# Reordering the opening loads of a one-core hybrid decoder step: three tiles of x, the first weights, then the rest of x

## Chip, cores and metric

The kernel runs on one core of one Trainium2 chip. The metric is the device time of one launch in microseconds (us); the median of several runs counts. The engines are TensorE (PE, with its weight loads PEld), VectorE (DVE), ScalarE (ACT), GpSimd (POOL) and SyncE (SP), which here only issues transfers.

## What is computed

One inference step of a one-layer decoder with two head groups (sparse attention and HGRN2), for a prompt of 1024 tokens and 8 sample tokens that share the weights. What matters here is only its beginning:

```
def _rmsnorm(x, g):
    x32 = x.astype(jnp.float32)
    y = x32 * lax.rsqrt(jnp.mean(x32 * x32, axis=-1, keepdims=True) + EPS)
    return (y * g.astype(jnp.float32)).astype(x.dtype)

z = _split(_rmsnorm(x, g_pre) @ w_in)     # x: (1024 + 8) x 1024, w_in: 1024 x 3864
f = lb + (1.0 - lb) * jax.nn.sigmoid(z['f_b'])
q = jax.nn.silu(z['q_b'])
```

`lb` is a softmax over `hg_lower`, two small rows of 512 numbers. Everything is float32.

## The kernel before

**Stages.** `project` loads and normalizes x, then makes ten products of x with slices of `w_in`, with the HGRN2 work between them; `attention` and `finish` follow. A float32 product is made of three products of rounded parts: x is split into `xhi` and `xlo`, each weight tile into `w_hi` and `w_lo`, and the products hi*hi, hi*lo and lo*hi are added up in PSUM.

**x.** `load_x` is a generator. It issues the loads of nine tiles (eight of 128 tokens with 1024 columns, 512 KB each, and one of 8 tokens), the first four into the later tile `V`, the others into `x_in` (tags AT, S and O of the HGRN pool). For each tile, ACT squares it and sums the squares (L200), DVE works out the inverse root in a chain of twelve operations on one column (L202, L79 to L84; `x_ss`, `rs_t`, `rs_g`, `x_rs`) and scales the tile (L214), TensorE transposes it in two halves of four 128x128 blocks (L218, two PSUM buffers `ph`), and ACT and DVE write `xhi` (L50) and `xlo` (L51). The sum of the next tile is asked for before the scaling of the present one.

**Weights.** `load_w` makes eight tiles (k = 0 to 7) of 128 rows and up to 512 columns: one transfer per column part into `w_raw` (three buffers), `w_hi` on ACT (L238), `w_lo` on DVE (L239). Tile k is loaded when buffer k - 3 has been split. The first product uses two parts of 256 columns, so sixteen transfers of 128 KB.

**First product.** `feat(..., groups_first=True)`: 4 feature blocks of 128 (two of f, two of q) in each of 3 token groups of 344 tokens, 24 matmuls of 344 columns each. Its evacuations allocate tiles F and K (two buffers each) and Q; F's needs `lb` and `oml`, which `consts2` works out from `hg_lower` (L145 to L154, tiles `hg_lo`, `hg_mx`, `hg_ex`). The transfers of `hg_lower`, issued by ACT, are put after the last x transfer in the order.

**Order of the work.** No engine's order is written by hand. A planner runs the program against a simulated clock, with the program's order as priority, and fixes the order of the instructions of each engine and of the issues of each queue; on the chip each engine keeps that order and waits in it. `after` only adds an order between two instructions. The page table (`pt_raw`, L648, eight transfers of 4-byte elements) belongs to a later part of the program.

Of the kernel before, what the change touches and what calls it, by code (L numbers as in the profile page):

```python
# [7 lines left out]
F32 = mybir.dt.float32  # L8
# [4 lines left out]
AF = mybir.ActivationFunctionType  # L13
OP = mybir.AluOpType
# [7 lines left out]
TS = T + NB  # L22
D = 1024
EPS = 1e-6
C_Q, C_KC, C_KS, C_KW, C_G, C_ZA, C_QB, C_FB, C_IB, C_ZB = 0, 512, 768, 1024, 1280, 1304, 1816, 2328, 2840, 3352


class Kernel:
# [148 lines left out]
    def load_x(self, ctx):  # L177
        nc, a = self.nc, self.a
        self.xhi = self.xpool.tile([128, 8, TS], F32R, name="xhi")
        self.xlo = self.xpool.tile([128, 8, TS], F32R, name="xlo")  # L180
        wk = self.pool(ctx, "xwork", bufs=2)
        xs, hp = [], self.hp
        four = hp.tile([128, 8, 512], F32, name="V", bufs=1).rearrange("p a b -> p (a b)")
        for i in range(9):
            n = 128 if i < 8 else NB
            if i < 4:
                x = four[:, i * D:(i + 1) * D]
            else:
                x = hp.tile([128, 8, 128], F32, name="x_in", tag=("AT", "S", "O")[(i - 4) // 2]).rearrange("p a b -> p (a b)")[:n]
            self.xdma = nc.sync.dma_start(x, a["x_prompt"][0, i * 128:i * 128 + n] if i < 8 else a["x_sample"][:, 0])  # L190
            xs.append((i, n, x))

        def norms(tiles):
            ss = wk.tile([128, 4], F32, name="x_ss")
            if tiles[-1] == 8:
                nc.gpsimd.memset(ss, 1.0)
            for j, t in enumerate(tiles):
                _, n, x = xs[t]
                junk = wk.tile([128, D], BF, name="x_sq")[:n]
                nc.scalar.activation(junk, x, AF.Square, accum_out=ss[:n, j:j + 1])  # L200
            ss = ss[:, :len(tiles)]
            nc.vector.tensor_scalar(ss, ss, 1.0 / D, EPS, op0=OP.mult, op1=OP.add)  # L202
            r = wk.tile([128, 4], F32, name="x_rs")[:, :len(tiles)]
            self.rsqrt(wk, r, ss)
            return r

        groups = [(i,) for i in range(9)]
        r = norms(groups[0])
        for gi, tiles in enumerate(groups):
            rn = norms(groups[gi + 1]) if gi + 1 < len(groups) else None  # L210
            for j, t in enumerate(tiles):
                i, n, x = xs[t]
                tok = slice(i * 128, i * 128 + n)
                nc.vector.tensor_scalar(x, x, r[:n, j:j + 1], None, op0=OP.mult)  # L214
                for h in range(2):
                    p = self.ps_h.tile([128, 512], F32, name="ph").rearrange("p (a b) -> p a b", a=4)
                    for k in range(4):
                        nc.tensor.transpose(p[:, k, :n], x[:, (4 * h + k) * 128:(4 * h + k + 1) * 128], self.ident[:n, :n])  # L218
                    self.split(self.xhi[:, 4 * h:4 * h + 4, tok], self.xlo[:, 4 * h:4 * h + 4, tok], p[:, :, :n],
                               nc.scalar, nc.vector)  # L220
            r = rn
            yield gi

    def load_w(self, src, *parts):

        nc = self.nc
        out = []
        width = sum(p[1] for p in parts)
        for k in range(8):
            raw = self.wpool.tile([128, 512], F32, name="w_raw", bufs=3)[:, :width]  # L230
            o = 0
            for c0, n in parts:
                dma = nc.sync.dma_start(raw[:, o:o + n], src[k * 128:(k + 1) * 128, c0:c0 + n])
                o += n
            hi = self.wpool.tile([128, 512], F32R, name="w_hi", bufs=9)[:, :width]
            lo = self.wpool.tile([128, 512], F32R, name="w_lo", bufs=9)[:, :width]
            g = self.gpre[:, k:k + 1]
            nc.scalar.activation(hi, raw, AF.Copy, scale=g)  # L238
            nc.vector.scalar_tensor_tensor(lo, raw, g, hi.bitcast(F32), op0=OP.mult, op1=OP.subtract)  # L239
            out.append((hi, lo))  # L240
        self.nload += 1
        for b in range(2 * self.nload - 4, 2 * self.nload - 2):
            if 0 <= b < NB:
                self.after(nc.sync.dma_start(
                    self.a["win_kv_sample"][0, b, :511].rearrange("s a h d -> s (a h d)"),
                    self.a["cache_win_kv"][0, b, 1:].rearrange("s a h d -> s (a h d)")), dma)
        return out

    def feat(self, *parts, groups_first=False, w=None, ps=None):

# [29 lines left out]
    def project(self, ctx):  # L280
        nc, a = self.nc, self.a
# [5 lines left out]
        hp = self.hp = self.pool(hctx, "hg", bufs=2)  # L287
        with ExitStack() as c:
            self.gpre = self.xpool.tile([128, 8], F32, name="gpre")
            nc.scalar.dma_start(self.gpre, a["g_pre"][0].rearrange("(k p) -> p k", p=128))  # L290
            self.nload = 0
            x = self.load_x(c)
            next(x)
            w0 = self.load_w(a["w_in"][0], (C_FB, 256), (C_QB, 256))
            for _ in x:
                pass
            self.consts2(c, mp)
# [5 lines left out]
        K, Q, F = {}, {}, {}  # L303
# [338 lines left out]
    def page_index(self, pool):  # L642

        nc = self.nc
        pt = self.a["page_table"]
        raw = pool.tile([128, NB], I32, name="pt_raw", bufs=1)
        for i in range(8):
            dma = nc.sync.dma_start(raw[16 * i:16 * i + 16], bass.AP(tensor=pt.tensor, offset=pt.offset + i, ap=[[0, 16], [8, NB]]))  # L648
            if i == 0:
                self.pidma = dma  # L650
        lane = pool.tile([128, NB], I32, name="pt_lane", bufs=1)
        nc.gpsimd.iota(lane, pattern=[[0, NB]], base=0, channel_multiplier=1)
        nc.vector.tensor_scalar(lane, lane, 15, None, op0=OP.bitwise_and)
        self.pidx = self.cp.tile([128, NB], I32, name="pidx")
        nc.vector.scalar_tensor_tensor(self.pidx, raw, 16.0, lane, op0=OP.mult, op1=OP.add)
# [738 lines left out]
```

## Time and profile before

| | |
|---|---|
| median of 3 runs | 1091.31 us (1091.28 to 1093.86) |
| profiled execution | 1092.95 us, span 1091.2 us |
| PE busy | 1051.9 us (96%) |
| DVE, ACT, POOL busy | 618.0, 388.5, 241.1 us |
| mean transfer rate | 107 GB/s |

PE is the engine that is busy nearly all the time. Matmuls overlap, so the spacing of their starts, not the duration of one, tells their pace.

### The profile page before, as it was taken

How to read it: one execution, taken by the hardware profiler on the slowest of the kernel's cores; microseconds unless marked ns; L12 is line 12 of the kernel's file. 1: busy time of each engine (PE TensorE's matmuls, PEld its weight loads, DVE VectorE, ACT ScalarE, POOL GpSimd, SP SyncE). 2: the span in 40 equal slices, each digit the busy share in tenths (PEclk: the TensorE clock that was granted, in tenths of full speed). 3: DMA queues.
4: the chain of work that ended last, by engine and by line, in shares of the span. 5: the costliest groups of instructions: out<-in, count | busy, mean ns of one | idle time of the engine just before them, and what ended most of it. 6: DMA issues, size and time to landing. Idle time of an engine off the chain costs nothing.

```text
span 1091.2 us, 18921 instructions
## 1 busy us (share of the span) xinstructions
PE 1051.9 (96%) x7021; PEld 936.8 (86%) x7021; DVE 618.0 (57%) x1822; ACT 388.5 (36%) x786; POOL 241.1 (22%) x276
## 2 busy tenths in 40 slices
PE   4999999999899899999989999999999999999998
PEld 3898799999789899999968898888788888778876
DVE  6847565666484535543574666766655677461223
ACT  4622234313133335432224544553554332241112
POOL 0024231331031133002023111111323133131111
PEclk9999999999999999999969999999999999999999
DMA  6212023333454666304468711001831474131110
GB/s 195 78 29 68 11 72 100 117 101 120 144 173 135 193 222 208 135 1 118 123 186 250 189 38 42 20 21 41 230 111 42 137 199 119 41 97 49 47 37 31
DMA packets 119007, 116.44 MB, mean 107 GB/s; under 512 B 18902, under 2 KB 101166, under 8 KB 116612
## 3 DMA queue, kind: packets, MB, share of 16 engines
q1 hardware_dynamic: 97412, 79.46, 25.6%
q10 hardware_dynamic: 19200, 19.01, 5.1%
q0 software_dynamic: 2304, 16.78, 4.6%
q8 instruction: 55, 0.90, 0.4%
q14 instruction: 36, 0.29, 0.1%
HBM read 84.84 MB, written 29.31 MB: 105 GB/s over the span
## 4 chain that ended last, share of the span: by engine, by line
PE 81%; DMA 9%; DVE 5%; issue 2%; ACT 1%; POOL 1%; SPq 0%; ACTq 0%; DVEq 0%; POOLq 0%
PE pa L42 37%; PE pb L42 27%; PE ph L42 9%; PE pt L42 4%; DMA vb<-v_d 2%; DMA w_raw<-w_in 2%; PE ph L714 1%; DMA w1r<-cmp_w 1%; DMA fw_raw<-w_out 1%; PE pa L1124 1%; DMA f_z<-oT_d 1%; DMA cg<-cache_cmp_kv,pidx 1%; DMA V<-x_prompt 1%; PE ph L1318 1%; DVE w_lo L239 1%
## 5 line engine op out<-in xcount | busy, mean ns | idle before, releaser
L42 PEld LDWEIGHTS pb<-V,P 128*128 128x128 f32 x1056 | 143.8, 194 | 11.8 <-POOL P L959 0.9
L42 PE MATMUL pb<-V,P 128*128 128x128 f32 x1056 | 149.2, 279 | 0.5 <-DVE mx L908 0.4
L42 PE MATMUL pa<-xhi,w_hi 128*128 128x344 f32 x384 | 125.7, 329 | 3.3 <-ACT w_hi L238 1.7
L42 PE MATMUL pa<-xlo,w_hi 128*128 128x344 f32 x384 | 124.2, 325 | 0.0
L42 PE MATMUL pa<-xhi,w_lo 128*128 128x344 f32 x384 | 123.3, 326 | 0.0
L954 ACT ACTIVATE P<-ph 128x512 f32<-128x512 f32 (+4 forms) x148 | 85.8, 595 | 100.4 <-PE ph L42 78.3
L915 DVE CUSTOM_DVE_ANT_0 junk<-pa,mask 128x320 bf16<-128x320 f32 (+5 forms) x150 | 73.1, 496 | 35.7 <-PE pa L42 35.1
L42 PE MATMUL pa<-w_lo,xhi 128*128 128x256 f32 (+2 forms) x256 | 79.8, 316 | 0.1
L42 PE MATMUL pa<-w_hi,xlo 128*128 128x256 f32 (+2 forms) x256 | 79.6, 315 | 0.0
L42 PE MATMUL pa<-w_hi,xhi 128*128 128x256 f32 (+2 forms) x256 | 78.9, 317 | 0.0
L42 PEld LDWEIGHTS pa<-xhi,w_hi 128*128 128x128 f32 x384 | 73.3, 191 | 5.0 <-ACT w_hi L238 2.4
L238 ACT ACTIVATE w_hi<-w_raw,gpre 128x512 fp32r<-128x512 f32 (+2 forms) x80 | 47.4, 616 | 78.1 <-DMA w_raw<-w_in 46.5
L42 PEld LDWEIGHTS pa<-xlo,w_hi 128*128 128x128 f32 x384 | 73.2, 191 | 0.1
L42 PEld LDWEIGHTS pa<-xhi,w_lo 128*128 128x128 f32 x384 | 72.7, 190 | 0.4 <-DVE w_lo L239 0.2
L42 PE MATMUL ph<-QA,KA 128*128 128x512 f32 (+4 forms) x148 | 66.4, 451 | 2.5 <-ACT P L954 2.5
L42 PE MATMUL pa<-KB,QB 65*128 65x320 f32 (+6 forms) x195 | 64.8, 369 | 1.1 <-DVE mx L915 0.7
L239 DVE SCALAR_TENSOR_TENSOR w_lo<-w_raw,gpre,w_hi 128x512 fp32r<-128x512 f32 (+2 forms) x80 | 51.4, 663 | 21.6 <-ACT w_hi L238 20.9
L42 PE MATMUL pa<-fw_hi,yh 128*128 128x512 f32 (+1 forms) x160 | 61.7, 385 | 0.0
L42 PE MATMUL pa<-fw_hi,yl 128*128 128x512 f32 (+1 forms) x160 | 61.6, 385 | 0.0
L42 PE MATMUL pa<-fw_lo,yh 128*128 128x512 f32 (+1 forms) x160 | 61.6, 385 | 0.0
L42 PE MATMUL ph<-QB,KB 68*128 68x512 f32 (+3 forms) x148 | 58.5, 405 | 0.0
L42 PE MATMUL pb<-x,w1h 128*128 128x384 f32 (+1 forms) x192 | 55.9, 353 | 0.3 <-ACT x L50 0.3
(457 smaller groups left out, 2391.3 us busy)
## 6 DMA issues: line engine op xcount, KB each, us to landing
w_raw<-w_in SPq DMA_DIRECT2D x32, 256.0 KB
w_raw<-w_in SPq DMA_DIRECT2D x48, 128.0 KB
VS<-sg SPq DMA_DIRECT2D x8, 512.0 KB
sg<-cache_win_kv SPq DMA_DIRECT2D x16, 256.0 KB
fw_raw<-w_out SPq DMA_DIRECT2D x16, 256.0 KB
fw_raw<-ple_gate SPq DMA_DIRECT2D x16, 256.0 KB
f_x<-x_prompt SPq DMA_DIRECT2D x8, 512.0 KB
win_kv_sample<-cache_win_kv SPq DMA_DIRECT2D x8, 511.0 KB
```

Of the source, the lines that this page charges most:

```text
L42: return self.nc.tensor.matmul(out, lhsT, rhs, start=start, stop=stop, skip_group_check=True)
L238: nc.scalar.activation(hi, raw, AF.Copy, scale=g)
L239: nc.vector.scalar_tensor_tensor(lo, raw, g, hi.bitcast(F32), op0=OP.mult, op1=OP.subtract)
L714: nc.tensor.transpose(pt[:, i * 128:(i + 1) * 128], src[b0 + j // 2, kv][:, j % 2, 2 * jp:2 * jp + 2].rearrange("p j d -> p (j d)"), self. ...
L915: nc.vector.tensor_tensor_reduce(junk, pm, mk, 1.0, -1e30, op0=OP.add, op1=OP.max, accum_out=o)
L954: nc.scalar.activation(P, ps, AF.Exp, scale=0.125)
L1124: nc.tensor.transpose(pt[:, j * 128:(j + 1) * 128], rows(j), self.ident)
L1318: nc.tensor.transpose(pt[:, c], h[:, k * 128:(k + 1) * 128], self.ident[:n, :n])
```

## The change

The x loads are issued in two parts with all sixteen first weight transfers between them. These weights go into four tiles of the HGRN pool that are not yet in use (tags F, F, K, K; two weight tiles in each). Tiles 1 and 2 of x share one norm. The first weights are split into hi and lo in two passes: 128 columns of all eight tiles, then 384 columns of all eight. The page-table transfers are put behind the last weight transfer that was issued before them in the program, which is that of the second product.

```diff
@@ load_x
                 x = hp.tile([128, 8, 128], F32, name="x_in", tag=("AT", "S", "O")[(i - 4) // 2]).rearrange("p a b -> p (a b)")[:n]
+            if i == 3:
+                yield
             self.xdma = nc.sync.dma_start(x, a["x_prompt"][0, i * 128:i * 128 + n] if i < 8 else a["x_sample"][:, 0])
             xs.append((i, n, x))
...
-        groups = [(i,) for i in range(9)]
+        groups = [(0,), (1, 2)] + [(i,) for i in range(3, 9)]
@@ load_w
-    def load_w(self, src, *parts):
+    def load_w(self, src, *parts, raws=None):
...
         for k in range(8):
-            raw = self.wpool.tile([128, 512], F32, name="w_raw", bufs=3)[:, :width]
-            o = 0
-            for c0, n in parts:
-                dma = nc.sync.dma_start(raw[:, o:o + n], src[k * 128:(k + 1) * 128, c0:c0 + n])
-                o += n
+            if raws:
+                raw = raws[k]
+            else:
+                raw = self.wpool.tile([128, 512], F32, name="w_raw", bufs=3)[:, :width]
+                o = 0
+                for c0, n in parts:
+                    dma = self.lastw = nc.sync.dma_start(raw[:, o:o + n], src[k * 128:(k + 1) * 128, c0:c0 + n])
+                    o += n
...
-            nc.scalar.activation(hi, raw, AF.Copy, scale=g)
-            nc.vector.scalar_tensor_tensor(lo, raw, g, hi.bitcast(F32), op0=OP.mult, op1=OP.subtract)
-            out.append((hi, lo))
+            if not raws:
+                nc.scalar.activation(hi, raw, AF.Copy, scale=g)
+                nc.vector.scalar_tensor_tensor(lo, raw, g, hi.bitcast(F32), op0=OP.mult, op1=OP.subtract)
+            out.append((hi, lo, raw, g))
+        for cs in ((slice(0, 128), slice(128, width)) if raws else ()):
+            for hi, lo, raw, g in out:
+                nc.scalar.activation(hi[:, cs], raw[:, cs], AF.Copy, scale=g)
+                nc.vector.scalar_tensor_tensor(lo[:, cs], raw[:, cs], g, hi[:, cs].bitcast(F32), op0=OP.mult, op1=OP.subtract)
...
-        return out
+        return [o[:2] for o in out]
@@ project
             next(x)
-            w0 = self.load_w(a["w_in"][0], (C_FB, 256), (C_QB, 256))
+
+            raws = []
+            for tag in ("F", "F", "K", "K"):
+                t = hp.tile([128, TS], F32, name="w0", tag=tag)
+                raws += [t[:, :512], t[:, 512:1024]]
+            for k, raw in enumerate(raws):
+                for o, c0 in ((0, C_FB), (256, C_QB)):
+                    nc.sync.dma_start(raw[:, o:o + 256], a["w_in"][0, k * 128:(k + 1) * 128, c0:c0 + 256])
+            for _ in range(2):
+                next(x)
+            w0 = self.load_w(None, (C_FB, 256), (C_QB, 256), raws=raws)
             for _ in x:
                 pass
@@ page_index
             dma = nc.sync.dma_start(raw[16 * i:16 * i + 16], bass.AP(tensor=pt.tensor, offset=pt.offset + i, ap=[[0, 16], [8, NB]]))
+            self.after(dma, self.lastw)
```

## Rows read from the trace of the kernel before

**Rows 1.** Busy time and share of the span, whole page.

```profile
PE 1051.9 (96%) x7021; PEld 936.8 (86%) x7021; DVE 618.0 (57%) x1822; ACT 388.5 (36%) x786; POOL 241.1 (22%) x276
```

**Rows 2.** Chain that ended last, first 70 us: start us, us, what.

```profile
2.19 8.22 DMA V<-x_prompt
...
20.75 7.21 DMA w_raw<-w_in
...
41.22 0.44 PE ph L218 x4
```

**Rows 3.** Busy windows of TensorE: stretch, length, busy, PEclk, DMA share, GB/s.

```profile
40.00:77.10 37.10, 37.10 (x244) 1.00 0.02 4
```

**Rows 4.** Timeline of TensorE: start us, us, line, operation.

```profile
21.04 1.23 PE L42 MATMUL pa<-xhi,w_hi 128*128 128x344 f32 x3 [1.00 <-ACT xhi L50]
...
24.21 0.49 PE L42 MATMUL pa<-xhi,w_lo 128*128 128x344 f32 x1
24.50 0.49 PE L42 MATMUL pa<-xhi,w_hi 128*128 128x344 f32 x1
...
25.39 0.32 PE L42 MATMUL pa<-xhi,w_hi 128*128 128x344 f32 x1
...
26.79 0.32 PE L42 MATMUL pa<-xhi,w_lo 128*128 128x344 f32 x1
28.82 0.42 PE L42 MATMUL pa<-xhi,w_hi 128*128 128x344 f32 x1 [1.71 <-ACT w_hi L238]
...
77.22 0.40 PE L42 MATMUL pa<-w_hi,xhi 128*128 128x512 f32 x1
```

**Rows 5.** Timeline of SP's queue: start us, us of issuing, transfer.

```profile
9.15 7.77 SPq L233 DMA_DIRECT2D w_raw<-w_in  x6
16.97 3.27 SPq L648 DMA_DIRECT2D pt_raw<-page_table  x7
20.36 63.76 SPq L233 DMA_DIRECT2D w_raw<-w_in  x18
```

**Rows 6.** Windows by transfer rate: last three columns PEclk, DMA share, GB/s.

```profile
2.00:8.00 6.00, 0.00 (x0) 0.00 (x0) 3.87 (x25) 2.98 (x6) 0.00 (x0) 1.00 0.83 260
8.00:14.00 6.00, 1.97 (x8) 1.57 (x8) 4.07 (x30) 2.83 (x8) 0.00 (x0) 1.00 1.03 408
14.00:17.00 3.00, 1.97 (x8) 1.55 (x8) 3.00 (x18) 1.51 (x4) 0.00 (x0) 1.00 1.05 237
18.50:25.50 7.00, 6.00 (x23) 4.87 (x23) 5.28 (x22) 3.58 (x8) 0.00 (x0) 1.00 0.05 0
```

**Rows 7.** Packets of all queues from 20 to 22 us.

```profile
DMA packets 235, 0.00 MB, mean 0 GB/s; under 512 B 235, under 2 KB 235, under 8 KB 235
```

**Rows 8.** Timeline of DVE: the norm chains of tiles 0 and 1.

```profile
8.16 0.15 DVE L202 TENSOR_SCALAR x_ss<-x_ss 128x1 f32<-128x1 f32 x1 [1.17 <-ACT x_sq L200]
...
9.38 0.16 DVE L84 SCALAR_TENSOR_TENSOR x_rs<-rs_t,rs_g 128x1 f32<-128x1 f32 x1
```

**Rows 9.** ACT's groups by form: count, busy us, mean ns, idle before.

```profile
L238 ACT ACTIVATE w_hi<-w_raw,gpre 128x512 fp32r<-128x512 f32 x16 | 11.0, 719 | 13.4 <-DMA w_raw<-w_in 13.4
L50 ACT CAST xhi<-ph 128x512 fp32r<-128x512 f32 x16 | 9.1, 581 | 4.3 <-PE ph L218 4.2
L601 ACT ACTIVATE o_sq<-O 128x128 bf16<-128x128 f32 x32 | 9.5, 299 | 0.2
L200 ACT ACTIVATE x_sq<-V 128x1024 bf16<-128x1024 f32 x4 | 4.2, 1056 | 6.2 <-DMA V<-x_prompt 3.0 <-DVE rs_t L82 2.8 <-DVE rs_t L83 0.3
```

**Rows 10.** DVE's groups by form, first 80 us.

```profile
L51 DVE TENSOR_TENSOR xlo<-ph,xhi 128x512 fp32r<-128x512 f32 x16 | 10.9, 684 | 2.0 <-ACT xhi L50 1.9
L239 DVE SCALAR_TENSOR_TENSOR w_lo<-w_raw,gpre,w_hi 128x512 fp32r<-128x512 f32 x12 | 8.9, 745 | 5.1 <-ACT w_hi L238 5.0
```

**Rows 11.** Timeline of all engines: issue and first reader of `hg_lo`.

```profile
7.99 2.82 ACTq L145 DMA_DIRECT2D hg_lo<-hg_lower  x2
...
17.74 0.15 DVE L147 TENSOR_TENSOR hg_mx<-hg_lo 128x4 f32<-128x4 f32 x1
```

## The prediction, as it went on record

> **What bounds the kernel now.** I read the page's first part, then the chain that ended last over the first 70 us, then the busy windows of TensorE, and last the timelines of each engine's opening. The page says that PE is busy for 96% of the span [rows 1]: whatever moves the moment from which PE runs without a gap moves the end. The chain shows that early on this moment is set by other things: x landing until 10.41 us (2.19 + 8.22), and later a weight tile that is issued at 20.75 us and lands only 7.21 us afterwards; by 41 us it is TensorE itself. In the window the reader is to see that PE is busy wholly from 40 us to 77.1 [rows 3]. The first product ends, and the next begins, at 77.22 [rows 4].
>
> Its own work is much smaller than 77 us. The product has 4 feature blocks x 3 token groups x 24 = 288 matmuls, which at speed start 0.157 us apart (from 25.39 to 26.79 there are 9 steps, 0.156 each [rows 4]), 45.2 us; eighteen half tiles of four transposes at 0.44 us (two of them smaller) make 7.9 us [rows 2]. That is 53.1 us, so 24.1 us of the 77.2 are waiting or a slower clock. Why weights are late is in the queue: SP issues all of x, then six weight parts, then seven page-table loads, and only then the rest of the weights [rows 5]. From 18.5 to 25.5 us the transfers move nothing (0 GB/s, busy share 0.05) [rows 6], while the page table's 4-byte packets go by at 235 in 2 us [rows 7]; the weights issued behind them wait.
>
> **Part 1: order of the loads.** Three tiles of x are 1.57 MB. From 2 to 8 us the transfers moved 260 GB/s, 1.56 MB, so the third lands at about 8.0 us, as now. Behind them now come the 16 weight parts, 2.10 MB. Price: the window 8 to 14 us ran at 408 GB/s with 512 KB loads, 14 to 17 us at 237 with weight parts and small packets mixed in [rows 6]. I take 350, nearer the first, because the small packets will not run beside the weights: 6.0 us, all landed at 14 us. Bounds: 5.1 us (408) and 8.9 us (237), 13 to 17 us. An issue of SP takes 0.47 us at most (seven in 3.27), and where it takes longer, as the six parts' 7.77 us, it waits for older transfers to land [rows 5]; sixteen are 7.5 us from 2.2 us on, no more than the transfers themselves need. The other five full tiles, 2.62 MB at 408, take 6.4 us: x3 lands at 15.3, x7 at 20.4, later than now by some 5 to 6 us. They are first needed for the second token group. What covers this: 96 matmuls of the first group, 15 us.
>
> The Trainium skill speaks against the small parts: its page "DMA: Bandwidth & Descriptors", section "Rules for kernel authors", wants at least 1 MiB per transfer for full bandwidth, and the section "Bandwidth" gives 138 GB/s at 64 KB. By that figure the weights would take an estimated 15 us and land at 23, and the first product would end near 79 us instead of the 71 of the sum below. The trace disagrees for queued transfers: 237 GB/s in a stretch with parts of 128 KB and smaller packets [rows 6].
>
> **Part 2: no buffer wait, page table later.** The weights go into idle F and K tiles, so none waits for one of three raw buffers, and no page table stands ahead of them; the wait of 7.21 us leaves the chain [rows 2]. The page-table loads go behind the next product's last weight. They would block that queue for the same 7 us there; covered, because the product that follows needs its weights some 45 us later (the token product between has 192 matmuls of 512 columns; at 512/344 of the spacing above an estimated 0.23 us each). I cost it at nothing; uncovered it is at most 7.
>
> **Part 3: joint norm of tiles 1 and 2.** It removes one chain of 12 small DVE operations (0.15 us each, about 0.1 apart: 13 of them start from 8.16 to 9.38 [rows 8]), some 1.2 us of DVE. It makes tile 1 wait for tile 2's squares, about 1 to 1.5 us. Now DVE stands idle for 1.17 us before tile 1's sum at 8.16, which was put into the middle of tile 0's chain [rows 8]. The same can happen with the joint sum, at worst until 9.4. Both are inside the time in which tile 2 sets the start.
>
> **Part 4: pieces of 128 and 384 columns.** 512 columns cost 0.72 us on ACT and 0.75 on DVE; for 128 columns the nearest row is 0.30 on ACT, and I take the same for DVE [rows 9, 10]. By a straight line 384 columns cost about 0.6 on each. So eight pairs cost 1.2 to 1.4 us more on each engine. In return the first feature block can start after eight 128-column pieces (2.4 us of each engine) and not after the whole 5.9. The 384 pieces are covered by the first block's 24 matmuls (3.8 us at speed, 6.9 at the slow clock), if they stand ahead of other work on ACT and DVE.
>
> **The start.** Tile 2 lands at 8.0; square and its sum 1.06 + about 0.2 [rows 9], 9.3; chain 1.3, 10.6; tile 1 is scaled at 11.4 and tile 2 at 12.1 (0.75 each). Then four half tiles through two PSUM buffers, each four slow transposes (twice 0.44 [rows 2]), cast 0.58, subtraction 0.68 [rows 9, 10], about 1.3 apart when overlapped: 16.5 us. The weights' first pieces fit in the gaps. Bounds: 14.5 (chain and halves perfectly packed, ACT free) and 20 (ACT and DVE, which are fixed in order, each held by one late transfer, as ACT was until 10.41 [rows 2]).
>
> **The clock.** The granted clock reads 1.00 from the first window [rows 6], but spacing says otherwise: matmuls of 344 columns start 0.285 us apart at 24.21 and 0.156 apart from 25.39, which is the 1.2 and the 2.4 GHz level; before it rose PE had been busy without a gap from about 21 us [rows 4]. I take the first 4 us of the new dense stretch at half rate, a loss of 2.0 us; bounds 0 (the transposes before it have raised it) and 3.1 (all 24 of the first block slow, 24 x 0.129).
>
> **Stalls.** ACT and DVE run in an order fixed beforehand on guessed landing times. Now this costs PE 1.7 us at 28.82, after ACT had stood at the weight that took 7.21 us [rows 4, 2]. I allow 2.0 us, bounds 0 and 6.
>
> **The sum.** 16.5 + 45.2 + 5.3 (twelve half tiles still to transpose) + 2.0 + 2.0 = 71.0 us for the end of the first product, against 77.2: 6.2 us earlier. From there PE runs on without a wait [rows 4], so I carry it whole. The profiled execution took 1092.95 us for a span of 1091.2, 1.64 over the median; it would become 1086.7, and the median **1085.1 us**, said as 1085. With all bounds good 14.5 + 50.5 = 65.0, 12.2 us less; with all bad 20 + 50.5 + 3.1 + 6 = 79.6, 2.4 us more.
>
> **Rivals.** A difference of 0.3%, 3.3 us, is about what a measurement of this kernel can tell from no change.
>
> *A, the lower-bound loads hold DVE (no change).* `hg_lo` is put behind the last x load, and so behind 16 weight parts. It is two loads of 512 packets of 4 bytes each; at 235 packets in 2 us they take 8.7 us [rows 7]. Issued now at 7.99 they were there before `hg_mx` at 17.74, which waited for nothing [rows 11]. Issued at 15 to 16 they land at 24 or 25. If `hg_mx` stands early in DVE's order, the 384-column subtractions and tile 3 stand behind it: PE finishes the first block at 22 and waits 4 us, and the clock may fall once more (2 us). Gain 0 to 1 us: 1090 to 1091. For it: the two issues already held ACT for 2.82 us [rows 11]. Against it: the planner may place `hg_mx` late, since its first reader is the first evacuation. Chance 0.2.
>
> *B, the same, later (slower).* If the issue waits for x7 at 20.4, `hg_lo` lands at 29. With `hg_mx` ahead of the subtractions PE idles from 22 to 30: 8 + 2 - 6.2 = 3.8 us slower, 1095. The point that decides is a landing after about 28 us with `hg_mx` ahead of the second weight pieces; against it stands that x7's slot is not the oldest. Chance 0.1.
>
> *C, the parts land slowly.* At the 237 GB/s of [rows 6] the weights are whole at 17 us, the last 128-column pieces a little later, the first block starts at 18 to 19, some 2 us later than forecast: 1087. Against it: the small packets that ran in that window will not run beside the weights. Chance 0.08. The rule of the Trainium skill named in part 1 pushes this way, and further than any row does.
>
> *D, the change does not do what it says.* Preparation of three tiles on ACT and DVE, not transfers, sets a start near 20 us and stalls stay: 1088 to 1093. Chance 0.07.
>
> *Forecast*: chance 0.55, own range 1080 to 1088. Range over the cases 1080 to 1093; it leaves out most of B and the best tail. Faster: 0.55 + 0.08 + 0.03 of D = 0.66. No change: 0.18 of A and 0.04 of D = 0.22. Slower: B's 0.1 and 0.02 of A, where its wait grows, = 0.12.
>
> **What the profile after would show.** SP: three x loads, sixteen weight parts without a gap longer than a landing, six x loads; no 0 GB/s stretch before 20 us. First product matmul near 16.5 us instead of 21.04, next product near 71 instead of 77.2. Spacing 0.285 until about 20.5. `hg_mx` with no idle time of DVE before it. The prediction is wrong if DVE or ACT shows one wait of several us between 15 and 30 us, or if the later stages give the gain back as new PE gaps after 80 us.

## The result, and the profile after

The changed kernel is 1.4% slower: a median of 1108.75 us (6 runs, 1105.44 to 1110.22) against 1092.28 us (6 runs, 1089.87 to 1094.32) for the kernel before, ratio 1.0139, 95% interval 1.0118 to 1.0159. The forecast was 1085, with a range of 1080 to 1093. The profiled execution took 1105.44 us (span 1103.7), 12.5 us more than that of before (it is the fastest of its six runs; the medians differ by 16.5).

First the start of the page of the changed kernel, which answers to [rows 1]. PE is as busy as before in us and a smaller share of a longer span.

```profile
PE 1050.9 (95%) x7021; PEld 935.5 (85%) x7021; DVE 618.5 (56%) x1818; ACT 390.8 (35%) x794; POOL 240.2 (22%) x276
```

SP's timeline after (start, us of issuing, transfer) answers to [rows 5]:

```profile
0.81 1.34 SPq L192 DMA_DIRECT2D V<-x_prompt  x3
2.20 10.26 SPq L311 DMA_DIRECT2D w<-w_in  x16
12.50 0.43 SPq L192 DMA_DIRECT2D V<-x_prompt  x1
...
16.48 72.16 SPq L238 DMA_DIRECT2D w_raw<-w_in  x8
88.69 1.28 SPq L254 DMA_DIRECT2D win_kv_sample<-cache_win_kv  x2
90.01 3.84 SPq L668 DMA_DIRECT2D pt_raw<-page_table  x7
94.84 8.62 SPq L238 DMA_DIRECT2D w_raw<-w_in  x4
```

The loads stand as the change says. The page table now stands ahead of the third product's weights, from 90.01 us. PE's timeline of the opening and of that later place (idle time and its releaser in brackets) answers to [rows 4]:

```profile
10.69 1.97 PE L220 MATMUL ph<-ident,V 128*128 128x128 f32 x8 [10.69 <-DVE V L216]
21.20 1.94 PE L220 MATMUL ph<-ident,V 128*128 128x128 f32 x8 [8.54 <-DVE rs_t L82]
23.69 1.11 PE L220 MATMUL ph<-ident,V 128*128 128x128 f32 x4 [0.55 <-DVE xlo L51]
27.70 1.12 PE L220 MATMUL ph<-ident,V 128*128 128x128 f32 x4 [2.90 <-DVE xlo L51]
29.57 1.23 PE L42 MATMUL pa<-xhi,w_hi 128*128 128x344 f32 x3 [0.75 <-ACT xhi L50]
...
81.74 0.40 PE L42 MATMUL pa<-w_hi,xhi 128*128 128x512 f32 x1
...
103.11 0.50 PE L42 MATMUL pa<-w_hi,xhi 128*128 128x512 f32 x1 [3.62 <-ACT V L349]
```

Two losses are to be seen. The first matmul comes at 29.57 us instead of 21.04, after a hole of 8.54 us and one of 2.90; the first product ends at 81.74 instead of 77.22. And at 103.11 PE, which had no wait in this region before, stands for 3.62 us. Why the first hole is there is in DVE's timeline, which answers to [rows 8 and 11]:

```profile
9.59 0.17 DVE L204 TENSOR_SCALAR x_ss<-x_ss 128x2 f32<-128x2 f32 x1 [1.18 <-ACT x_sq L202]
...
10.81 0.16 DVE L80 TENSOR_SCALAR rs_g<-rs_t 128x2 int32<-128x2 int32 x1
10.88 0.87 DVE L250 SCALAR_TENSOR_TENSOR w_lo<-w,gpre,w_hi 128x384 fp32r<-128x384 f32 x2
11.67 0.15 DVE L82 TENSOR_TENSOR rs_t<-rs_g 128x2 f32<-128x2 f32 x1
11.74 0.87 DVE L250 SCALAR_TENSOR_TENSOR w_lo<-w,gpre,w_hi 128x384 fp32r<-128x384 f32 x2
...
17.25 1.40 DVE L250 SCALAR_TENSOR_TENSOR w_lo<-w,gpre,w_hi 128x384 fp32r<-128x384 f32 x3
18.57 0.15 DVE L82 TENSOR_TENSOR rs_t<-rs_g 128x2 f32<-128x2 f32 x1
...
19.85 0.15 DVE L204 TENSOR_SCALAR x_ss<-x_ss 128x1 f32<-128x1 f32 x1 [1.13 <-ACT x_sq L202]
...
20.11 0.16 DVE L84 SCALAR_TENSOR_TENSOR x_rs<-rs_t,rs_g 128x2 f32<-128x2 f32 x1
...
21.04 0.75 DVE L216 TENSOR_SCALAR V<-V,x_rs 128x1024 f32<-128x1024 f32 x1
...
26.88 0.16 DVE L147 TENSOR_TENSOR hg_mx<-hg_lo 128x4 f32<-128x4 f32 x1 [3.11 <-DMA hg_lo<-hg_lower]
```

DVE hardly waits, it is busy with the wrong thing. The joint chain of twelve small steps, 1.3 us for one tile before, takes from 9.59 to 20.11, because the planner put the sixteen `w_lo` pieces, mostly a pair at a time, between its steps (a group such as "128x384 x2" joins one piece of 128 columns and one of 384). Two `xlo` of tile 0 stand there too, and near the end the sum of tile 3, for which DVE waits 1.13 us. ACT is filled likewise with sixteen `w_hi` pieces, the last done at 16.90. Tiles 1 and 2 are scaled at 20.30 and 21.04. Then `hg_mx` waits for `hg_lo`, in front of the next `xlo`. The late place in ACT's timeline:

```profile
91.01 0.72 ACT L244 ACTIVATE w_hi<-w_raw,gpre 128x512 fp32r<-128x512 f32 x1 [3.86 <-DMA w_raw<-w_in]
102.08 0.51 ACT L244 ACTIVATE w_hi<-w_raw,gpre 128x256 fp32r<-128x256 f32 x1 [10.34 <-DMA w_raw<-w_in]
102.49 1.05 ACT L349 COPY V<-pa 128x512 f32<-128x512 f32 x2
```

The third product's first weight, issued at 94.84 behind the page table, is split at 102.08. In ACT's order this split stands ahead of the evacuations of the running product (L349), so these wait with it, and PE stops until the evacuation of `V` is done (the releaser in its line at 103.11).

### The profile page after: what moved, and what is told of

It reads as the page before. It is cut to its first block, busy times and chain, and to the rows that moved or that the text cites. A ratio compares the mean times of both kernels' runs of the same rounds, so it can differ in the third digit from the quotient of the medians.

```text
span 1103.7 us, 18912 instructions
## 1 busy us (share of the span) xinstructions
PE 1050.9 (95%) x7021; PEld 935.5 (85%) x7021; DVE 618.5 (56%) x1818; ACT 390.8 (35%) x794; POOL 240.2 (22%) x276
## 4 chain that ended last, share of the span: by engine, by line
PE 80%; DMA 9%; DVE 6%; issue 2%; ACT 2%; POOL 0%; SPq 0%; ACTq 0%; DVEq 0%; POOLq 0%
PE pa L42 37%; PE pb L42 27%; PE ph L42 9%; PE pt L42 4%; DMA vb<-v_d 2%; DMA w_raw<-w_in 2%; DMA fw_raw<-w_out 1%; PE ph L735 1%; PE pa L1145 1%; DMA fw_raw<-ple_gate 1%; DMA hg_lo<-hg_lower 1%; DVE w_lo L245 1%; DMA V<-x_prompt 1%; ACT w_hi L249 1%; DMA f_z<-oT_d 1%
## 5 line engine op out<-in xcount | busy, mean ns | idle before, releaser
L244 ACT ACTIVATE w_hi<-w_raw,gpre 128x512 fp32r<-128x512 f32 (+2 forms) x72 | 42.0, 605 | 78.6 <-DMA w_raw<-w_in 45.6
L245 DVE SCALAR_TENSOR_TENSOR w_lo<-w_raw,gpre,w_hi 128x512 fp32r<-128x512 f32 (+2 forms) x72 | 47.7, 686 | 23.0 <-ACT w_hi L244 22.1
L42 PE MATMUL ph<-QB,KB 68*128 68x512 f32 (+4 forms) x148 | 59.0, 407 | 0.0
```

What stands on the lines that cost most here:

```text
L42: return self.nc.tensor.matmul(out, lhsT, rhs, start=start, stop=stop, skip_group_check=True)
```

## The experiments

The theories that the expectations name: **D**, the pieces in DVE's order set the late start; **T**, the late lower-bound loads set it; **P**, the page table costs its place wherever it stands in SP's queue; **L**, the later stages lose time of their own. Rivals that occur once are explained in the expectations. The experiments ran in groups on several chips, each group beside runs of the kernel before on the same chip (medians 1091.5 to 1094.1 us); a ratio is to those, in the row "after" to the six runs of the section above. Since totals of one kernel spread over 10 us and more, the stages are read from marks in each profile: the first matmul of the first product, its end, SP's issue of `v_d`, and the last store of y that ACT issues (one more, issued by SP, follows some 3.5 us later in each), from the PE and SP timelines and the stores' groups. Each mark is that of one profiled execution.

| kernel | first matmul | first product ends | `v_d` issued | from there to ACT's last y | ratio to before, 95% interval |
|---|---|---|---|---|---|
| before | 21.04 | 77.22 | 139.8 | 945.0 | |
| before, again | 20.56 | 76.88 | 139.5 | 943.4 | 1.0025 [0.9996, 1.0053] |
| after | 29.57 | 81.74 | 149.8 | 947.4 | 1.0139 [1.0118, 1.0159] |
| after, again | 29.86 | 82.15 | 150.7 | 942.4 | 1.0122 [1.0064, 1.0180] |
| e1_pt_back | 29.11 | 81.96 | 144.6 | 952.9 | 1.0066 [1.0036, 1.0096] |
| e2_before_pt | 20.53 | 73.39 | 141.9 | 943.0 | 1.0011 [0.9978, 1.0045] |
| e3_hold384 | 23.42 | 79.05 | 146.8 | 945.3 | 1.0065 [1.0035, 1.0096] |
| e4_hg_early | 27.62 | 80.36 | 148.8 | 944.0 | 1.0125 [1.0066, 1.0185] |
| e5_before_ptpool | 27.91 | 80.87 | 143.6 | 948.1 | 1.0032 [0.9997, 1.0068] |
| e5b_before_ptact | 24.20 | 77.95 | 140.6 | 946.9 | 1.0017 [0.9997, 1.0036] |
| e6_scale_hold | 26.29 | 81.02 | 149.5 | 944.8 | 1.0128 [1.0055, 1.0201] |
| e7_order_only | 27.51 | 81.65 | 151.0 | 946.1 | 1.0118 [1.0042, 1.0195] |
| e9_all_hold | 32.72 | 86.55 | 149.2 | 943.5 | 1.0083 [1.0051, 1.0115] |
| f1_before_pt1 | 20.58 | 73.29 | 135.9 | 945.4 | 1.0005 [0.9983, 1.0027] |
| f2_hold_hg_pt1 | 24.22 | 76.85 | 139.5 | 948.5 | 1.0013 [0.9991, 1.0034] |
| f3_joint_pt1 | 20.93 | 73.98 | 136.6 | 953.7 | 0.9992 [0.9962, 1.0022] |

**The page table, back and alone.** e1 is the changed kernel without the new order of the page table; e2 is the kernel before with nothing but that order.

```diff
# e1
-            self.after(dma, self.lastw)
# e2, in load_w and page_index of before
-                dma = nc.sync.dma_start(raw[:, o:o + n], src[...])
+                dma = self.lastw = nc.sync.dma_start(raw[:, o:o + n], src[...])
...
+            self.after(dma, self.lastw)
```

> The changed kernel without the one added order, so that the page-table loads go back in front of the fourth weight tile of the second product. Theory P (the moved page table blocks the third product's first weight, ACT stands at it, PSUM fills, PE idles 3.6 us at 99 to 103 us and runs at the slow clock to 107): this gap goes, 5 to 8 us faster than the changed kernel, 1101 to 1104. Theory S (the late start of the first product is the whole loss): within 2 us of the changed kernel, 1107 to 1110.

> The kernel before with the moved page table as its only change. Theory P: the opening gains, since the weights no longer stand behind the page table (start of the dense stretch 3 to 6 us earlier), and the third product's first weight is late by 7 us, which costs 5 to 6 us near 95 us: 1089 to 1095, with a new PE gap there. Theory S (moving the page table is harmless): 3 to 6 us faster than before, 1086 to 1089, no gap.

In e1 PE is busy without a hole there, and `v_d` comes at 144.6 instead of 149.8: the page table's place is worth 5.2 us, give or take the 0.9 by which this mark differs between two profiles of the changed kernel. All engines' windows, after and e1 (stretch, length, busy us of PE, PEld, DVE, ACT and POOL, then PEclk, DMA share, GB/s):

```profile
90.00:100.00 10.00, 9.49 (x42) 7.37 (x40) 5.31 (x9) 0.72 (x1) 2.29 (x1) 1.00 0.39 118
100.00:110.00 10.00, 6.89 (x23) 5.47 (x24) 3.90 (x5) 3.52 (x6) 2.38 (x1) 0.83 0.17 53
```

```profile
90.00:100.00 10.00, 10.00 (x45) 8.11 (x44) 6.61 (x11) 2.96 (x6) 4.45 (x2) 1.00 0.51 175
100.00:110.00 10.00, 10.00 (x45) 8.08 (x44) 5.91 (x6) 3.03 (x4) 3.83 (x3) 1.00 0.01 2
```

Where e1's seven loads went is in its SP timeline: behind three weights of the second product, which nobody wants until the first product ends. The first product ended as in the changed kernel, so in this place they cost nothing that can be seen.

```profile
17.04 4.29 SPq L238 DMA_DIRECT2D w_raw<-w_in  x3
22.36 4.79 SPq L668 DMA_DIRECT2D pt_raw<-page_table  x7
28.10 60.75 SPq L238 DMA_DIRECT2D w_raw<-w_in  x5
```

e2 shows both sides in the kernel before: the first product ends at 73.39, 3.8 us earlier, since the opening has no page table; then PE has a hole of 4.0 us behind 90 us, and by `v_d` it is 2.1 us later, so the new place costs 5.9. P holds in both directions.

**The pieces, and the lower bound.** e3 orders the 384-column pieces of ACT, and with them those of DVE, behind tile 2's split; e6 orders only DVE's behind tile 2's scaling; e4 takes the order of the `hg_lower` loads behind x away.

```diff
# e3
+                    self.xsplit = self.split(self.xhi[...], self.xlo[...], p[:, :, :n],
...
+                act = nc.scalar.activation(hi[:, cs], raw[:, cs], AF.Copy, scale=g)
+                if cs.start:
+                    self.after(act, self.xsplit)
# e6
+                self.xscale = nc.vector.tensor_scalar(x, x, r[:n, j:j + 1], None, op0=OP.mult)
...
+                dve = nc.vector.scalar_tensor_tensor(lo[:, cs], ...)
+                if cs.start:
+                    self.after(dve, self.xscale)
# e4
-            self.after(nc.scalar.dma_start(lo[:, r], a["hg_lower"][r]...), self.xdma)
+            nc.scalar.dma_start(lo[:, r], a["hg_lower"][r]...)
```

> The changed kernel with the 384-column pieces ordered behind tile 2's split. Theory D (on DVE the 384-column pieces stand between the steps of the joint norm, which ends at 20.3 us instead of 11): the norm of tiles 1 and 2 ends near 15 us, the first product's matmuls start near 21 instead of 29.6 us, 6 to 8 us faster than the changed kernel, 1100 to 1103. Theory T (late transfers, hg_lower and x, set the start): start within 2 us of 29.6, 1107 to 1110.

> The changed kernel with one edit: the 384-column subtractions on VectorE are ordered behind the scaling of tile 2; ScalarE's pieces and everything else stay. Theory D (pieces planned between the steps of the joint norm set the start): eight pieces of 0.55 us leave the chain, so x_rs comes near 16 us instead of 20.1, bounded by the last 128-column piece, which waits for weights until 16; first matmul 24 to 25.5 instead of 29.6, first product ends 77 to 79 instead of 81.7, total 3 to 4.5 us below the changed kernel, near 1102 to 1105. Theory T (the late lower-bound loads set it): hg_mx still waits 2 to 3 us near 27 and the first matmul stays at 28 to 30.

> The changed kernel with the two hg_lower loads no longer ordered behind the last x load. Theory T: the 3.1 us for which DVE stands at hg_mx at 23.8 to 26.9 us leave the path, first product 3 us earlier, 1105 to 1106. Theory D alone: the 3 us are taken up by the work behind it, and 1024 small packets beside the first x loads delay tiles 0 to 2 by 1 to 2 us: 1108 to 1111.

In e3 the first matmul comes at 23.42, 6.2 us earlier. But only 2.7 us of it are left at the end of the first product: now `xhi` and `xlo` of the later tiles are late, PE waits for them for 0.54 us at 42.57 and 1.64 us at 44.79, and its granted clock from 40 to 50 us is 0.83. In e6 the chain does what D says:

```profile
13.38 0.15 DVE L84 SCALAR_TENSOR_TENSOR x_rs<-rs_t,rs_g 128x2 f32<-128x2 f32 x1
...
14.19 1.41 DVE L216 TENSOR_SCALAR V<-V,x_rs 128x1024 f32<-128x1024 f32 x2
15.51 2.99 DVE L250 SCALAR_TENSOR_TENSOR w_lo<-w,gpre,w_hi 128x384 fp32r<-128x384 f32 x6
18.42 0.68 DVE L51 TENSOR_TENSOR xlo<-ph,xhi 128x512 fp32r<-128x512 f32 x1
19.02 2.19 DVE L250 SCALAR_TENSOR_TENSOR w_lo<-w,gpre,w_hi 128x384 fp32r<-128x384 f32 x5
...
26.67 0.16 DVE L147 TENSOR_TENSOR hg_mx<-hg_lo 128x4 f32<-128x4 f32 x1 [3.68 <-DMA hg_lo<-hg_lower]
```

Tiles 1 and 2 are scaled from 14.19 on, 6.1 us earlier, and yet the first matmul gains only 3.3 us: the pieces that left the chain now stand in front of `xlo`, and then T's wait comes, 3.68 us at 26.67. The expected start of 24 to 25.5 and end of 77 to 79 are missed. e4 shows T alone: its edit brings 2.0 us of the start and 1.4 us of the product, not the 3 us expected. The edit has a price of its own: `hg_mx` now stands in tile 0's chain and waits 2.09 us there (tile 0 is scaled at 11.42 instead of 9.88), and beside the two loads the transfers from 8 to 14 us run at 255 GB/s where the changed kernel has 299. Neither D nor T alone holds the loss; each hides part of the other.

**Is it the joint norm or the pieces' width?** e7 keeps of the change only the load order, the idle tiles and the page table's place: single norms, one pass of 512 columns.

```diff
-        groups = [(0,), (1, 2)] + [(i,) for i in range(3, 9)]
+        groups = [(i,) for i in range(9)]
...
-        for cs in ((slice(0, 128), slice(128, width)) if raws else ()):
+        for cs in ((slice(0, width),) if raws else ()):
...
-            for _ in range(2):
+            for _ in range(3):
                 next(x)
```

> The changed kernel with single norms and one pass of 512 columns: of the change only the order of the loads, the idle tiles and the page table's place are left. If the joint norm and the split into pieces are to blame for the late start (rival J), the first matmul comes at 22 to 25 us and the first product ends near 75 to 77. If it is the early weights as such, whose splits the fixed order puts ahead of tile 2's norm whatever their width (theory D in its wide form), the first matmul stays at 28 to 31 and the first product ends at 80 to 83, total within 3 us of the changed kernel.

Start 27.51, product 81.65: the product is where wide D puts it, the start half a us before its window and far from J's 22 to 25, so the rival J falls for the most part. Eight whole `w_lo` stand between the steps of the single norms, and tile 2 is scaled at 21.69 (21.04 with the joint norm and the pieces). Weights that are there early are split early, whatever their width, and tile 2's norm stands behind them.

**Another queue for the page table.** e5 and e5b are the kernel before with the eight loads issued by GpSimd and by ScalarE; e9 is the changed kernel with all `w_lo` pieces and ACT's 384 pieces behind tile 2's scaling, `hg_lower` at once, and the page table on GpSimd's queue.

```diff
# e5 (e5b: nc.scalar)
-            dma = nc.sync.dma_start(raw[16 * i:16 * i + 16], ...)
+            dma = nc.gpsimd.dma_start(raw[16 * i:16 * i + 16], ...)
# e9, beside that and e4's edit
+                self.after(dve, self.xscale)
+                if cs.start:
+                    self.after(act, self.xscale)
...
-            self.after(dma, self.lastw)
```

> The kernel before with one edit: the eight page-table loads are issued by GpSimd's queue and no longer by SyncE's. Theory Q (the 4-byte loads hold up only what stands behind them in their own queue): the stretch of 0 GB/s in the opening goes, the first product ends near 73.4 us, as where the page table stood behind the second product's weights, and nothing is paid later: the issue of v_d comes near 136 us instead of 139.8, total 3 to 5 us below before, 1087 to 1090 where before has 1093. Rival S (4-byte packets slow all queues, wherever they are issued): the first product still ends at 76 to 78 us, total as before within 2 us.

> The changed kernel with four edits: all VectorE weight pieces and ScalarE's 384-column pieces are ordered behind the scaling of tile 2, hg_lower is loaded at once, the page table goes to GpSimd's queue without an order. If theories D, T and Q together hold all of the loss: scaling of tile 2 near 13 us, first matmul 18 to 21, first product ends 71 to 75, no gap of TensorE at 100 to 105 us, issue of v_d at 134 to 138, total 1086 to 1090 where before has 1093. If the later stages lose 4 us whatever the opening does (theory L), the total is 1090 to 1094 with the same v_d.

> The kernel before with the eight page-table loads on ScalarE's hardware queue. On GpSimd's queue, beside the x loads, the transfers fell to 82 to 152 GB/s from 8 to 16 us. If 4-byte packets slow their neighbours whatever the queue (theory S): the same fall to below 200 GB/s between 4 and 16 us, first product ends at 79 to 83 us, total 2 to 6 us above before. If it is the software queue of GpSimd alone (theory G): 350 GB/s or more at 8 to 12 us, as before, where the lower-bound loads ran beside x; first product ends at 73 to 76, unless the lower-bound loads, now behind the page table in ScalarE's queue, come late and hg_mx waits.

Theory Q, that only the own queue is held up, falls. The transfers from 8 to 14 us (last column GB/s), in e5, and then in e5b:

```profile
8.00:14.00 6.00, 1.97 (x8) 1.57 (x8) 2.57 (x19) 0.07 (x1) 0.00 (x0) 1.00 0.31 116
```

```profile
8.00:14.00 6.00, 1.97 (x8) 1.57 (x8) 4.45 (x32) 2.35 (x5) 0.00 (x0) 1.00 0.71 257
```

Before it was 408 [rows 6]. Beside the small loads of GpSimd the x loads crawl at 116 GB/s, and the first product ends at 80.87 instead of the expected 73.4, later than S expected too. On ScalarE's queue the harm is smaller: 257 GB/s, product 77.95, between the figures of S and of G. e9 has 42 GB/s in the same window, with both the page table and `hg_lower` there; its start of 32.72, far from the expected 18 to 21, says nothing on D and T, only on these small loads.

**Everything repaired.** f1 is the kernel before with the page table loaded in two transfers of 128 rows of 128 bytes, which stand behind `v_d` in SP's order (136.26 and 143.14 us), and the columns picked out by sixteen multiply-adds. f2 is e3 with e4's edit and that page table. f3 is f1 with the joint norm.

```diff
# f1, page_index
-        for i in range(8):
-            dma = nc.sync.dma_start(raw[16 * i:16 * i + 16], bass.AP(..., ap=[[0, 16], [8, NB]]))
+        for h in range(2):
+            raw = pool.tile([128, 32], I32, name="pt_raw", bufs=1)
+            dma = nc.sync.dma_start(raw, bass.AP(tensor=pt.tensor, offset=pt.offset + 32 * h, ap=[[0, 128], [1, 32]]))
...
+            for i in range(8):
+                nc.vector.scalar_tensor_tensor((self.pidx if i == 7 else lane)[:, 4 * h:4 * h + 4], rv[:, i], sel[:, i:i + 1],
+                                               lane[:, 4 * h:4 * h + 4], op0=OP.mult, op1=OP.add)
# f3, beside it
+        groups = [(0,), (1, 2)] + [(i,) for i in range(3, 9)]
```

> The kernel before with another form of the page table: instead of eight loads of 4-byte elements, two loads of 128 rows of 128 bytes, both behind v_d, and a choice of the columns by sixteen small multiply-adds on VectorE; no page-table load stands in the opening. Theory P (the 4-byte loads cost their place, wherever they stand in SyncE's queue): the first product ends near 73.4 us, no gap of TensorE at 90 to 110, issue of v_d near 136 instead of 139.8, total 3 to 5 us below before, ratio 0.995 to 0.998. Rival R (what the opening gains is given back before v_d by the next weights, whose loads depend on buffers and not on the page table): v_d stays at 139 to 141 and the total as before within 1.5 us.

> The changed kernel with three repairs: the 384-column pieces behind tile 2's split, hg_lower loaded at once, the page table in the form of two loads behind v_d. If theories D, T and P hold all of the loss: no wait at hg_mx after 20 us, first matmul 20 to 22.5 us, first product ends 74.5 to 77 us, no gap of TensorE at 100 to 105, issue of v_d 136 to 139, total 1088 to 1092 where before has about 1093. If the loss is in the load order itself (weights in 16 parts ahead of x3 to x8 land late, theory O), the first matmul may come at 21 but TensorE waits again before 60 us, first product 78 to 80, total 1095 or more.

> The kernel before with the page table in two loads behind v_d, and the joint norm of tiles 1 and 2; load order, buffers and whole weight tiles as before. The joint norm alone against the kernel with the page table moved (first matmul 20.58, first product 73.29, v_d 135.9): theory J0 (without weight pieces between its steps the joint norm is worth about nothing: 12 small operations of VectorE less, 1.2 us, against tile 1 waiting for tile 2's squares): first matmul 19.5 to 21.5, first product 72.3 to 74.3. Rival J1 (the joint chain is itself a loss, since transposes of tile 1 start later and TensorE has nothing in between): first matmul 22 to 24, first product 75 to 77. For the total, theory W (a gain in the opening is carried whole): 1088 to 1090 where before has 1092.5; theory V (the later stages give most of it back, in a granted clock lower by 0.001 to 0.002 or in another planned order): within 1.5 us of before.

f2 brings the changed kernel from 149.8 to 139.5 at `v_d`, level with before (139.8), and from a ratio of 1.0139 to 1.0013: repairs of D, T and P together take the loss against before away. But its start of 24.22 and `v_d` lie outside the expected 20 to 22.5 and 136 to 139, and the same page table brings before itself to 135.9 (f1): against f1 f2 still loses 3.6 us. Where they go is to be seen in ACT and DVE of f2, first ACT, then DVE:

```profile
16.68 0.40 ACT L249 ACTIVATE w_hi<-w,gpre 128x128 fp32r<-128x128 f32 x1 [0.85 <-DMA w<-w_in]
...
19.53 1.06 ACT L202 ACTIVATE x_sq<-V 128x1024 bf16<-128x1024 f32 x1 [2.44 <-DMA V<-x_prompt]
```

```profile
17.12 0.35 DVE L252 SCALAR_TENSOR_TENSOR w_lo<-w,gpre,w_hi 128x128 fp32r<-128x128 f32 x1 [0.90 <-ACT w_hi L249]
17.39 1.41 DVE L216 TENSOR_SCALAR V<-V,x_rs 128x1024 f32<-128x1024 f32 x2
```

Even the 128-column pieces stand in the chain, and the last waits for weights until 17; then ACT waits until 19.53 for tile 3 of x, which is behind the sixteen parts, in front of tile 1's `xhi`. f1, with all x first, starts at 20.58 and ends its product at 73.29, 3.6 us ahead of f2: with the page table out of the way, the old kernel's opening is the better one. Not all of the 3.6 us need be the load order's: f2 also has e4's edit with its price (254 GB/s from 8 to 14 us; `hg_mx` waits 2.42 us in tile 0's chain), and e3, without that edit, starts at 23.42. f1 gains no more in the opening than e2, 73.29 against 73.39, so there it is the place of the page table that counts; its four-byte form behind `v_d` was not tried. The joint norm alone (f3) is worth about nothing, 20.93 and 73.98.

**Both kernels once more.**

> The kernel before, unchanged, profiled on the chip of the other experiments. Theory N (the marks of one execution before v_d are the kernel's own, those after it vary): first matmul 20.5 to 21.5, first product 76.7 to 77.7, v_d 139.3 to 140.3, and from v_d to the last store of y 943 to 950 us. If v_d itself lies at 137 to 138 here (theory Z), the kernels with the moved page table gained only 1.5 to 2 us in the opening and nothing was given back. Ratio 1.000 within 0.003.

> The changed kernel, unchanged, on the chip of the other experiments. Theory N: first matmul 29 to 30, first product 81.2 to 82.2, v_d 149.3 to 150.3; from v_d to the last store of y 943 to 950, so that the part of the loss behind v_d is nothing but the spread of single executions. If the changed kernel loses a part of its own behind v_d (theory L), that stretch is 948 or longer again in the median execution and the total is 14 us or more above before, ratio 1.013 to 1.016; without such a part the ratio is 1.008 to 1.011.

The kernels are the unchanged two, on a chip of their own. The marks up to `v_d` repeat within 0.9 us, and Z falls. After, again, needs 942.4 us behind `v_d`, less than any other profile, but it is the fastest of its four runs, and its ratio of 1.0122 lies between what L (1.013 to 1.016) and its absence (1.008 to 1.011) would make. Its median is 13.9 us above that of before, `v_d` 11.2 us later; in the first runs it was 16.5 and 10.0. In e7 and e9, with `v_d` 11.2 and 9.4 us later, the medians are 11.5 and 9.4 above, which speaks against L. So L is not shown, and not excluded for the changed kernel. The unchanged kernel before read 1.0025 of itself, nearly as much as f1 and f3 could have gained: their 3.9 and 3.2 us at `v_d`, more than the marks' spread, would make 0.9964 and 0.9971. f1's interval, from 0.9983, leaves that out; f3's, from 0.9962, does not. Whether f1's gain is given back behind `v_d` stays open. No version beat the kernel before by more than such a spread.

## Why the prediction was wrong

**The size of the miss.** The profile was to become 1086.7 us and became 1105.44, 18.7 more: 10.7 in the first product (81.74 against 71.0), 5.2 for the page table (e1), and 2.8 left. The stretches behind `v_d` spread from 942.4 to 953.7 us over sixteen profiles, so 2.8 us in one profile show no third cause; the larger difference of the medians leaves one possible.

**The start: the step that failed.** I worked out 16.5 us, with "The weights' first pieces fit in the gaps" and bounds of 14.5 to 20; it was 29.57. The scaling of tile 2 ended at 21.79 (21.04 + 0.75) instead of 12.1, 9.7 of the 13.1 us; the rest is behind that, where DVE stood 3.11 us at `hg_mx`. I had priced the pieces and the chain, each rightly (a pair of 128 and 384 is 0.87 us by its group), but added them as if DVE would do the urgent one first. Its order is fixed by a plan on guessed landing times, and in it all sixteen pieces stand ahead of the end of a 1.3 us chain. I had even named that ACT and DVE are held by fixed order in the bound of 20, but only by one late transfer, not by work that is ready and not urgent. Before, the late arrival of the weights had kept them out of the norms: the load order that I took for a fault was also what set the priorities. In the timeline of the kernel before, tile 2 is scaled ahead of the first weight split:

```profile
16.33 0.75 DVE L214 TENSOR_SCALAR V<-V,x_rs 128x1024 f32<-128x1024 f32 x1
...
18.04 0.73 ACT L238 ACTIVATE w_hi<-w_raw,gpre 128x512 fp32r<-128x512 f32 x1
```

**Part 2.** The wait for three raw buffers and the 7.21 us left the chain, as said, and the gain of taking the page table away is real (e2, f1: 3.8 to 3.9 us). What failed is "covered, because the product that follows needs its weights some 45 us later" and "I cost it at nothing". The next weights in the queue were not that product's but the first of the one after. SP was done with the second product's last weight only at 88.64, issued the page table from 90.01, and came to these at 94.84, with ACT's evacuations behind them. Cost 5.2 us in after and 5.9 in e2, under the "at most 7" that I had written and left out of the bounds of the sum.

**Part 1** was nearly right: sixteen parts issued from 2.20 to 12.46, the last `w_hi` piece done by 16.9, inside 13 to 17 us, at 299 GB/s from 8 to 14 us where I had taken 350; but tile 3 of x came later than the 15.3 I gave it (ACT waited for it until 18.95 to 19.53 in e4, e6 and f2), and that cost f2 part of its start. From the 138 GB/s at 64 KB in the Trainium skill ("DMA: Bandwidth & Descriptors", section "Bandwidth", measured there for transfers issued by GpSimd) I had estimated that the weights land at 23; the trace disagrees, with all `w_hi` pieces done by 16.9. **Part 3**: about nothing, as costed (f3). **Part 4**: the widths were no matter (e7); "if they stand ahead of other work" was the wrong condition, since they did, and that was the loss.

**Clock and stalls.** From the first matmul the product took 52.2 us (81.74 - 29.57) where I had 54.5: so, if the matmuls and transposes took what I priced, these two terms were 2.3 us too large together.

**Rivals.** A and B named a true wait: `hg_lo` issued at 18.71, landed at 26.78 (chain below), 3.11 us of DVE, and worth 1.4 us at the end of the product (e4, net of that edit's own price). Most of the loss came through something else. D named the right engines, ACT and DVE, and the wrong size.

```profile
18.71 8.07 DMA hg_lo<-hg_lower
```

The two signs that I gave of a wrong prediction, a wait of several us on DVE between 15 and 30 and a new hole of PE after 80 us, both came.

## What to carry to other kernels

Work that arrives earlier is also done earlier: where an in-order engine runs by a plan, ask for each load that is moved forward which ready but not urgent instructions now stand in front of the chain that sets the start, and give those an order behind it. A slow load that is moved behind "the last" transfer stands in front of the next one: look for the first wait behind its new place, and put it where the loads behind it have the most slack (here behind the second product's first weights). And keep loads of single elements out of the opening: with the page table moved behind `v_d` as a few rows, the first product ended 3.9 us earlier (f1), though the total shows no gain.

## What the runs showed of the hardware

**Small loads beside large ones.** From 8 to 14 us, seven loads of 4-byte elements on GpSimd's queue brought the x loads of SP's queue from 408 to 116 GB/s, on ScalarE's to 257; with none of the seven in the opening, in f1, it was 406. From 2 to 8 us, beside the same loads, it was 243 and 267 against 260, so the rate falls only late; what makes it fall no row shows. The Trainium skill says in "DMA: Bandwidth & Descriptors", section "Issuing engines are not separate DMA queues", that transfers of all three issuers run on the same 16 engines and interleave; the runs agree in so far as loads of one queue slowed those of another, 408 to 116 and 257 GB/s.

**Here the clock fell after the hole, not in it.** PE's timeline after its hole of 3.62 us:

```profile
103.45 0.40 PE L42 MATMUL pa<-w_lo,xhi 128*128 128x512 f32 x1
103.69 0.40 PE L42 MATMUL pa<-w_hi,xlo 128*128 128x512 f32 x1
...
104.16 0.57 PE L42 MATMUL pa<-w_lo,xhi 128*128 128x512 f32 x1
104.53 0.63 PE L42 MATMUL pa<-w_hi,xlo 128*128 128x512 f32 x1
...
107.09 0.63 PE L42 MATMUL pa<-w_hi,xhi 128*128 128x512 f32 x1
107.51 0.45 PE L42 MATMUL pa<-w_lo,xhi 128*128 128x512 f32 x1
107.80 0.39 PE L42 MATMUL pa<-w_hi,xlo 128*128 128x512 f32 x1
108.03 0.40 PE L42 MATMUL pa<-w_hi,xhi 128*128 128x512 f32 x1
```

The first matmuls after it start 0.24 us apart, at the level of 2.4 GHz; from about 104.5 to 107.5 they are 0.43 apart, at that of 1.2 GHz, and then 0.23 again. The granted clock from 100 to 110 us is 0.83. By these spacings the slow stretch adds an estimated 1.6 us (nine steps in 3.64 us from 104.16 to 107.80, against 0.23 each) to the hole of 3.62, near the 5.2 that e1 gives.
